# Hybrid decoder layer on one core: other start addresses in SBUF for matmul operands, no work on the empty state, and a square root in the last rows

## The chip, the cores and the metric

The kernel runs on one core of a Trainium2 chip. The metric is device time in microseconds. TensorE (PE) multiplies, with its weight loads shown apart as PEld; VectorE (DVE), ScalarE (ACT) and GpSimd (POOL) do the elementwise work; SyncE (SP) issues DMAs. SBUF is the memory on the chip that all of them read, PSUM the one that TensorE writes.

## The reference

A layer for 2048 tokens of width 1024, float32:

```
u    = rmsnorm(x) * w_mix
proj = u @ w_in
# 4 HGRN2 heads of 128: a gated linear recurrence, computed in chunks
S_t  = diag(f_t) S_{t-1} + k_t v_t^T ;  o_t = S_t^T q_t ;  S_0 = 0
# 8 attention heads of 64, 2 key/value heads, window 128, a sink logit per head
h    = x + concat(rmsnorm(o_hg) * silu(g), o_att) @ w_out
v    = rmsnorm(h) * w_ffn
gate = causal_conv3(v @ w_gate) + conv_b          # 2816 channels
h    = h + (silu(gate) * (v @ w_up)) @ w_down
out  = rmsnorm(h) * w_final
```

The state S starts empty, so the first chunk has no product with it, and the state after the last chunk is not needed.

## The kernel before

**Precision.** Large products are computed from a high and a low part of each operand (both of type float32r, `split_into`: a cast on ScalarE, a subtraction on VectorE). A product is thus a triple of matmuls: high weight by high input, high weight by low input, low weight by high input (lines 734 to 736 in gate and up, 921 to 923 in down, 202 in the projections). Each loads a weight block of 128 columns and streams 512 columns.

**Stages.** The tokens are taken in two halves of 1024 (`hf`). Each half goes through the heads and attention (`hgrn`, `attend`; their stages are woven together by the list `ORDER`), the output projection (`out_proj`), gate and up (`gate_up`: 11 pairs of feature tiles, each with one gate unit and one up unit) and `down`.

**Gate, up and down by Strassen's scheme.** A unit of two feature tiles and two halves of tokens is made of seven products instead of eight (`pair_unit`). Their weights are the blocks A11, A12, A22, the difference S3, and the combinations S1, S2 and S4, which `prep_pair` makes on VectorE. A11, A12, S3 and A22 lie in ring buffers `whi` and `wlo`. The combinations are allotted by the helper `m` from the slots of tag `m`, eight of 1024 floats, which other tiles (`x`, the heads' q, the residual `h`, `y`, one weight pair of the output projection) also use: `S` holds the sums, `Sh` and `Sl` the high and low parts of S1 and S2, `S4` both parts of S4. (The profile calls these `S`, `Sh`, `Sl` and, for `S4`, `S` again.) The first pair of each half uses other homes: the buffers `ga` for `Sh` and `Sl`, and `dd`. `down` uses the two `ga` buffers as a third home for weights, `gad`, high part in the first and low part in the second.

**Where a tile starts.** A pool lays its tiles one behind another in each partition, so a tile's start follows from the sizes of those before it, rounded up to 32 bytes. In the built program before, the tiles that 512-wide matmuls read start 64 bytes past a multiple of 128, except: the second `ga` buffer (96 past), `dd` (0 past). From `F64` in the heads' pool on, starts are 32 past, which holds for `v`, `SS`, `sc` and the scores' `qh` and `ql`.

**The state.** `hgrn` transposes K by chunks into `Kn` (`pkn`), multiplies by v (`pu`), and accumulates in `SS`; the output `po` of a chunk adds the product of Q with the state before it. Before, this is done for all eight chunks of both halves, with a zeroed `state` at first.

**The last rows.** `last_rows` makes the last products of the second half by rows of 128 tokens (`tb` 0 to 3): ScalarE squares and sums a row block, VectorE forms the inverse root by an integer estimate and three Newton steps on 128x1 tiles, and scales the rows on their way out.

Within this, the scheduler of the language's tile layer sets each engine's final order from data dependences and its own timing model.

Of the kernel before, what the change touches and what calls it, by code (L numbers as in the profile page):

```python
# [17 lines left out]
P = 128  # L18
D = 1024
KT = D // P  # L20
S = 2048
HALF = 1024
NH = S // HALF
TT = HALF // P
# [5 lines left out]
FT = FF // P  # L30
EPS = 1e-6
PIECES = [2, 2, 2, 2, 2, 1]
OPS = ["B11", "T1", "B21", "T2", "T3", "B22", "T4"]
QUADS = ["A11", "A12", "A21", "A22"]
PRODUCTS = [("P1", "A11", "B11"), ("P5", "S1", "T1"), ("P6", "S2", "T2"), ("P3", "S4", "B22"),
            ("P7", "S3", "T3"), ("P2", "A12", "B21"), ("P4", "A22", "T4")]
AFTER = {2: 'po'}
ORDER = ("f0 q0 l0 qa0 v0 s0 sc0 w0 pv0 p0 f1 q1 l1 g0 pw0 w1 qa1 g1 sc1 f2 s1 q2 p1 qa2 m0 pv1 pw1 l2 v1 "
         "s2 sc2 f3 m5 q3 g2 p2 pv2 pw2 qa3 m6 m1 sc3 l3 m4 m2 s3 g3 pv3 p3 pw3").split()
UP_AFTER = 'T2'  # L40
LEVELS = [1, 2, 4, 8, 16, 32, 64]
NEG = -1.0e30
UT = 7
# [5 lines left out]
def hymba_layer(ctx: ExitStack, tc: tile.TileContext, a: dict, out: bass.AP, rows_out: bass.AP):  # L49
    nc = tc.nc  # L50
# [6 lines left out]
    cp = pool("const")  # L57
    xp = pool("x")
    wp = pool("w")
    hp = pool("h")  # L60
# [13 lines left out]
        return [(b, slice(b * 512, (b + 1) * 512)) for b in range(NB)]  # L74


    nmw = cp.tile([P, KT], F32, name="nmw")
    nc.scalar.dma_start(nmw, a["norm_mix_w"])
    ones = cp.tile([P, P], F32, name="ones")
    nc.vector.memset(ones, 1.0)  # L80
    warm = cp.tile([P, 1], F32, name="warm")
    nc.scalar.activation(warm, ones[:, 0:1], AF.Sigmoid)
    ident = cp.tile([P, P], F32, name="ident")
    nc.gpsimd.memset(ident, 1.0)
    nc.gpsimd.affine_select(out=ident, in_=ident, compare_op=ALU.is_equal, fill=0.0,
                            base=0, pattern=[[-1, P]], channel_multiplier=1)
    state = cp.tile([P, HG, P], F32, name="state")
    nc.vector.memset(state, 0.0)
    halo = cp.tile([P, FT, 2], F32, name="halo")
    nc.vector.memset(halo, 0.0)  # L90
    kc = cp.tile([P, 2, P], F32R, name="kcarry")
# [5 lines left out]
    marks = {}  # L97
# [350 lines left out]
    def hgrn(hf, h, X, invb, vs, WG, gates, mix, p, fu=None):  # L448

        fu = fu or unit(a["w_f"][h], X, "f")  # L450
        f = p.tile([P, HALF], F32, tag="f", name="f", bufs=2)
# [12 lines left out]
        Q = p.tile([P, HALF], F32, tag="Q", name="Q", bufs=2)  # L464
# [27 lines left out]
        F = f  # L492
        for m in LEVELS:
            nb = HALF // (2 * m)
            pl = ps("hg", "plev")
            if m < 32:
                n, nu = 64 // m, TT // 2
                far, near = [[512 - m, 2], [P, nu], [2 * m, n], [1, m]], [[512 + m, 2], [P, nu], [2 * m, n], [1, m]]
                G = p.tile([P, 512], F32, tag="G", name="G", bufs=2)
                nc.scalar.copy(across(G, 0, [[m, 2], [P, nu], [2 * m, n], [1, m]]), across(K, 0, near))  # L500
                for u in range(nu):
                    marks[m] = nc.tensor.matmul(across(pl, u * 64, [[256, 2], [1, 64]]), G[:, u * P:(u + 1) * P],
                                                across(Q, u * P + m, [far[0]] + far[2:]), start=True, stop=True)
                nf = P // m
                Kv, Qv = across(K, 0, near), across(Q, m, far)
                Fk = across(F, 1, [[4 * nf - 1, 2], [nf, nu], [2, n], [0, m]])
                Fq = across(F, 0, [[4 * nf + 1, 2], [nf, nu], [2, n], [0, m]])
                nc.vector.tensor_tensor(Kv, Kv, Fk, op=ALU.mult)
                nc.vector.tensor_tensor(Qv, Qv, Fq, op=ALU.mult)
            else:  # L510
                Qv = Q.rearrange("p (b w m) -> p b w m", w=2, m=m)
                Kv = K.rearrange("p (b w m) -> p b w m", w=2, m=m)
                for c in range(TT):
                    for s0 in range(0, P, 2 * m):
                        nc.tensor.matmul(pl[s0:s0 + m, c * m:(c + 1) * m], K[:, c * P + s0:c * P + s0 + m],
                                         Q[:, c * P + s0 + m:c * P + s0 + 2 * m], start=True, stop=True)
                Fv = F.rearrange("p (b w) -> p b w", w=2)
                nc.vector.tensor_tensor(Qv[:, :, 1], Qv[:, :, 1], Fv[:, :, 0:1].to_broadcast([P, nb, m]), op=ALU.mult)
                nc.vector.tensor_tensor(Kv[:, :, 0], Kv[:, :, 0], Fv[:, :, 1:2].to_broadcast([P, nb, m]), op=ALU.mult)
            Fv = F.rearrange("p (b w) -> p b w", w=2)  # L520
            Fn = p.tile([P, nb], F32, tag=f"F{m}", name=f"F{m}", bufs=1)
            nc.vector.tensor_tensor(Fn, Fv[:, :, 0], Fv[:, :, 1], op=ALU.mult)
            F = Fn
            if m < 32:
                mk = C.lmask[m].bitcast(U32).rearrange("p s t -> p (s t)")
                nc.vector.copy_predicated(across(ST.rearrange("p c t -> p (c t)"), m, far),
                                          across(mk, 0, [[64, 2], [0, nu], [m, n], [1, m]]),
                                          pl.rearrange("p (s u b m) -> p s u b m", s=2, u=nu, m=m))
                continue
            for s0 in range(0, P, 2 * m):  # L530
                nc.scalar.copy(ST[s0:s0 + m, :, s0 + m:s0 + 2 * m],
                               pl[s0:s0 + m, 0:TT * m].rearrange("p (c m) -> p c m", c=TT))
        yield
        v = vs[h]

        Kn = p.tile([P, TT, P], F32, tag="t4", name="Kn", bufs=2)
        for b in range(NB):
            pk = ps("hg", "pkn")
            for i in range(4):
                c = slice((b * 4 + i) * P, (b * 4 + i + 1) * P)  # L540
                nc.tensor.transpose(pk[:, i * P:(i + 1) * P], K[:, c], ident)
            nc.scalar.copy(Kn[:, 4 * b:4 * b + 4].rearrange("p a b -> p (a b)"), pk)
        SS = p.tile([P, TT, P], F32, tag="SS", name="SS", bufs=1)
        for b in range(NB):
            pu = ps("hg", "pu")
            for i in range(4):
                c = 4 * b + i
                marks["pu"] = nc.tensor.matmul(pu[:, i * P:(i + 1) * P], Kn[:, c], v[:, c], start=True, stop=True)
            for i in range(4):
                c = 4 * b + i  # L550
                prev = state[:, h] if c == 0 else SS[:, c - 1]
                nc.vector.scalar_tensor_tensor(SS[:, c], prev, F[:, c:c + 1], pu[:, i * P:(i + 1) * P],
                                               op0=ALU.mult, op1=ALU.add)
# [4 lines left out]
        po = [ps("hg", "po") for _ in range(NB)]  # L558
        for c in range(TT):
            cs = slice(c * P, (c + 1) * P)  # L560
            prev = state[:, h] if c == 0 else SS[:, c - 1]
            o = po[c // 4][:, c % 4 * P:(c % 4 + 1) * P]
            nc.tensor.matmul(o, ST[:, c], v[:, c], start=True, stop=False)
            marks["po"] = nc.tensor.matmul(o, Q[:, cs], prev, start=False, stop=True)
            nc.scalar.activation(on[:, c], o, AF.Square, accum_out=ss[:, c:c + 1])
        rs = rsqrt(ss, TT, 1.0 / P)
        if h == HG - 1:
# [6 lines left out]
        for b, bs in halves():  # L574
# [5 lines left out]
            else:  # L580
                nc.vector.scalar_tensor_tensor(blocks(g[:, bs]), blocks(pt, b), C.hgw, blocks(g[:, bs]),
                                               op0=ALU.mult, op1=ALU.mult)
            if h == HG - 1:
                hi, lo = mix[h]
                nc.scalar.copy(hi[:, bs], g[:, bs])
                nc.vector.tensor_tensor(lo[:, bs], g[:, bs], hi[:, bs].bitcast(F32), op=ALU.subtract)
        nc.vector.tensor_copy(state[:, h], SS[:, TT - 1])
        yield

    def project_v(hf, pr, X, rs, p):  # L590
# [91 lines left out]
    def prep_pair(src1, src2, home=None, ut=None, raws=None):  # L682
# [6 lines left out]
                    wp.tile([P, D], F32R, tag="lo", name="wlo", bufs=2))  # L689

        def m(name, shape=[P, D], dt=F32R):
            return hp.tile(shape, dt, tag="m", name=name, bufs=KT)

        A = None if home else ring()
        if A:
# [2 lines left out]
        if home:  # L698
            S1, S2, S4 = [ut(n) for n in ("S1", "S2", "S4")]
        else:  # L700
            S = m("S", [P, D], F32)
            S1, S2, S4 = S[:, lo], S[:, hi], r1[:, hi]
# [62 lines left out]
    def gate_up(hf, ops, hs, nxt, p):  # L765
# [5 lines left out]
        for pr in range(FT // 2):  # L771
            f0 = 2 * pr
            W, nxt = nxt, None
            ga = [p.tile([P, 2 + HALF], F32, tag="ga", name="ga", bufs=2) for _ in range(2)]

            def gate(i, j, x, y):
                dst = ga[i][:, 2 + j * 512:2 + (j + 1) * 512]
# [20 lines left out]
            for i in range(2):  # L798
# [3 lines left out]
                y = slot("y")  # L802
# [191 lines left out]
    def last_rows(hf, hh, st, fw, ready, pieces, p, then):  # L994
# [6 lines left out]
        def small(name):  # L1001
            return sp.tile([P, 1], F32, tag=name, name=name)

        for tb in range(4):
            ts = slice(tb * P, (tb + 1) * P)
            o = ps("mm", "rows")
# [27 lines left out]
            nc.scalar.activation(sq, o, AF.Square, accum_out=ss)  # L1034
            ms, mh, y, t = small("msr"), small("mhr"), small("yr"), small("tr")
            nc.vector.tensor_scalar(ms, ss, 1.0 / D, base[:, tb:tb + 1], op0=ALU.mult, op1=ALU.add)
            yi = y.bitcast(I32)
            nc.vector.tensor_scalar(yi, ms.bitcast(I32), 1, None, op0=ALU.logical_shift_right)
            nc.vector.tensor_scalar(yi, yi, -1.0, float(0x5F3759DF), op0=ALU.mult, op1=ALU.add)
            nc.vector.tensor_scalar(mh, ss, -0.5 / D, half[:, tb:tb + 1], op0=ALU.mult, op1=ALU.add)  # L1040
            for _ in range(3):
                nc.vector.tensor_scalar(t, y, y, mh, op0=ALU.mult, op1=ALU.mult)
                nc.vector.tensor_scalar(y, t, 1.5, y, op0=ALU.add, op1=ALU.mult)
            r = sq
# [130 lines left out]
```

## Time and profile before

| | |
|---|---|
| median of 3 runs | 2183.36 us (2181.68 to 2183.84) |
| the profiled execution | 2181.92 us |
| its span | 2179.9 us |
| granted TensorE clock, mean | 0.999 |
| TensorE busy | 2162.5 us, 99% |
| VectorE busy | 1630.9 us, 75% |
| ScalarE busy | 1049.7 us, 48% |
| HBM read, written | 195.37 MB, 57.15 MB |

"Busy" counts the time in which at least one instruction of an engine is under way. A group's row in the profile ends in count, busy time, mean duration of one in ns, and idle time of the engine just before. In the timeline a row begins with its start and its duration in us. A matmul is shown from its start to its modelled end, and the next one starts before that end; the time that a matmul takes of TensorE is the distance from one start to the next.

### The profile page before, as it was taken

What the parts mean: (1) busy time and instruction counts of PE and PEld (TensorE: products, weight loads), DVE (VectorE), ACT (ScalarE), POOL (GpSimd) and SP (SyncE); (2) the same over time, 40 slices, a digit from 0 to 9 for tenths busy, and PEclk for the clock granted to TensorE, in tenths of its full rate; (3) what the DMA queues carried; (4) which work ended last, traced back from release to release, by engine and by line L of the source; (5) the groups of instructions that cost most, each with busy time, mean ns of one, the idle gap of its engine ahead of it and who ended that gap; (6) DMA issues with size and microseconds to landing.
All of it is one profiled execution on the core that took longest, in us unless ns stands there. A gap on an engine that the chain in (4) does not pass through costs nothing.

```text
span 2179.9 us, 29020 instructions
## 1 busy us (share of the span) xinstructions
PE 2162.5 (99%) x11211; PEld 1813.3 (83%) x11211; DVE 1630.9 (75%) x2458; ACT 1049.7 (48%) x1825; POOL 15.8 (1%) x37
## 2 busy tenths in 40 slices
PE   8999999999999999999999999999999999999998
PEld 7988988888888888888889889888888888888887
DVE  6566668689787878785865666677888888787865
ACT  6445456554444445335635365445644444443452
POOL 2000000000000000000000000000000000000000
PEclk9999999999999999999999999999999999999999
DMA  4111112413232334964641010114232323259743
GB/s 156 40 30 39 30 39 69 135 59 126 92 115 93 99 118 152 384 227 152 205 135 30 30 49 22 50 61 143 70 116 87 129 84 124 86 190 393 232 145 131
DMA packets 91146, 254.41 MB, mean 117 GB/s; under 512 B 11136, under 2 KB 13952, under 8 KB 91008
## 3 DMA queue, kind: packets, MB, share of 16 engines
q1 hardware_dynamic: 90576, 252.29, 34.6%
q8 instruction: 88, 1.44, 0.3%
q14 instruction: 50, 0.41, 0.1%
q10 hardware_dynamic: 432, 0.27, 0.0%
HBM read 195.37 MB, written 57.15 MB: 116 GB/s over the span
## 4 chain that ended last, share of the span: by engine, by line
PE 97%; DVE 1%; ACT 1%; DMA 1%; issue 0%; SPq 0%; DVEq 0%
PE pop L202 8%; PE X L734 7%; PE X L735 7%; PE X L736 7%; PE q L202 4%; PE g L202 4%; PE f L202 4%; PE hq L202 4%; PE Y L735 4%; PE Y L734 4%; PE Y L736 4%; PE pdx L922 3%; PE pdx L921 3%; PE pdx L923 3%; PE pdy L922 3%; PE pdy L921 3%
## 5 line engine op out<-in xcount | busy, mean ns | idle before, releaser
L609 ACT CAST whi<-raw 128x1024 fp32r<-128x1024 f32 x88 | 92.6, 1053 | 103.1 <-PE X L735 68.5
L805 DVE SCALAR_TENSOR_TENSOR y<-ga,cw,y 128x1024 f32<-128x1024 f32 x88 | 112.6, 1282 | 37.7 <-ACT y L803 37.7
L736 PE MATMUL X<-T,wlo 128*128 128x512 f32 x352 | 137.0, 389 | 0.0
L735 PE MATMUL X<-T,whi 128*128 128x512 f32 x352 | 136.9, 389 | 0.0
L734 PE MATMUL X<-T,whi 128*128 128x512 f32 x352 | 136.9, 389 | 0.0
L610 DVE TENSOR_TENSOR wlo<-raw,whi 128x1024 fp32r<-128x1024 f32 x88 | 107.5, 1221 | 5.7 <-ACT whi L609 5.7
L183 ACT CAST whi<-raw 128x1024 fp32r<-128x1024 f32 x58 | 60.6, 1050 | 102.6 <-PE g L202 22.4
L740 ACT COPY u<-X 128x512 f32<-128x512 f32 x88 | 51.8, 588 | 97.8 <-PE X L736 97.7
L610 DVE TENSOR_TENSOR xld<-raw,xhd 128x1024 fp32r<-128x1024 f32 x72 | 81.1, 1133 | 8.1 <-ACT xhd L609 7.9
L609 ACT CAST xhd<-raw 128x1024 fp32r<-128x1024 f32 x72 | 69.5, 979 | 32.5 <-DMA raw<-act1B 9.6
L202 PE MATMUL pop<-XH,wlo 128*128 128x512 f32 x256 | 83.7, 392 | 0.8 <-DVE wlo L184 0.8
L202 PE MATMUL pop<-XL,whi 128*128 128x512 f32 x256 | 83.8, 391 | 0.0
L202 PE MATMUL pop<-XH,whi 128*128 128x512 f32 x256 | 83.4, 396 | 0.2
L184 DVE TENSOR_TENSOR wlo<-raw,whi 128x1024 fp32r<-128x1024 f32 x58 | 70.4, 1218 | 12.3 <-ACT whi L183 12.3
L734 PEld LDWEIGHTS X<-T,whi 128*128 128x128 f32 x352 | 66.1, 188 | 13.8
L735 PEld LDWEIGHTS X<-T,whi 128*128 128x128 f32 x352 | 66.1, 188 | 13.7
L736 PEld LDWEIGHTS X<-T,wlo 128*128 128x128 f32 x352 | 66.1, 188 | 13.7
L740 ACT COPY s<-X 128x512 f32<-128x512 f32 x44 | 25.9, 590 | 106.3 <-PE X L736 106.3
L602 PE MATMUL pvv<-whi,XL 128*128 128x256 f32 x256 | 73.5, 289 | 0.0
L601 PE MATMUL pvv<-whi,XH 128*128 128x256 f32 x256 | 73.1, 287 | 0.0
L603 PE MATMUL pvv<-wlo,XH 128*128 128x256 f32 x256 | 72.1, 284 | 0.0
L734 PE MATMUL X<-T,Sh 128*128 128x512 f32 x176 | 68.7, 390 | 0.0
(389 smaller groups left out, 6555.6 us busy)
## 6 DMA issues: line engine op xcount, KB each, us to landing
wr<-in_w_down SPq DMA_DIRECT2D x90, 512.0 KB, 5.3
raw<-in_w_gate SPq DMA_DIRECT2D x44, 512.0 KB, 3.6
raw<-in_w_up SPq DMA_DIRECT2D x44, 512.0 KB, 3.6
raw<-act0T SPq DMA_DIRECT2D x20, 512.0 KB, 5.7
raw<-act1T SPq DMA_DIRECT2D x20, 512.0 KB, 5.0
act0B<-y SPq DMA_DIRECT2D x33, 256.0 KB, 2.3
act1B<-y SPq DMA_DIRECT2D x33, 256.0 KB, 2.2
raw<-in_w_out SPq DMA_DIRECT2D x16, 512.0 KB, 3.6
```

The source lines that it names most:

```text
L202: nc.tensor.matmul(o[b], w, x[:, bs], start=f, stop=l)
L601: nc.tensor.matmul(o[:, 0:256], xh[:, t], hi[:, c], start=kt == 0, stop=False)
L602: nc.tensor.matmul(o[:, 0:256], xl[:, t], hi[:, c], start=False, stop=False)
L609: nc.scalar.copy(h, src)
L610: return (eng or nc.vector).tensor_tensor(l, src, h.bitcast(F32), op=ALU.subtract)
L734: nc.tensor.matmul(o, wh[:, ws], xh, start=i == 0 and not more, stop=False, skip_group_check=more)
L735: nc.tensor.matmul(o, wh[:, ws], xl, start=False, stop=False, skip_group_check=more)
L736: nc.tensor.matmul(o, wl[:, ws], xh, start=False, stop=i == 3, skip_group_check=more)
L740: nc.scalar.copy(t, o)
L805: nc.vector.scalar_tensor_tensor(y, g[:, w:w + HALF], C.cw[:, ft, w:w + 1], y, op0=ALU.mult, op1=ALU.add)
L921: nc.tensor.matmul(o, wh[:, i, c], ah[:, i, cols], start=f, stop=False, skip_group_check=more)
L922: nc.tensor.matmul(o, wh[:, i, c], al[:, i, cols], start=False, stop=False, skip_group_check=more)
```

## The change

1. The small tiles `nmw` and `warm`, and the tiles `F64`, become larger, and `ga` buffers get 4224 bytes instead of 4104. In the built program the tiles that matmuls read in the heads, `ga`'s second buffer and `dd` now start 64 bytes past a multiple of 128.
2. The slots of tag `m` are 4128 bytes apart instead of 4096, and their eight starts are 64, 96, 0, 32, 64, 96, 0 and 32 past a multiple of 128. `Sl` and `S4` begin 16 bytes into theirs.
3. The first chunk of the first half makes no product with the state, and the last chunk of the second half makes no transpose, product, sum or copy of the state. The memset of `state` goes.
4. In the last rows, the integer estimate and two of three Newton steps give way to a square root on ScalarE and a reciprocal on VectorE, with a warm-up of the root at the start of `last_rows`.

```diff
+GA = 1056
-    nmw = cp.tile([P, KT], F32, name="nmw")
+    nmw = cp.tile([P, 16], F32, name="nmw")[:, 0:KT]
-    warm = cp.tile([P, 1], F32, name="warm")
+    warm = cp.tile([P, 32], F32, name="warm")[:, 0:1]
-    nc.vector.memset(state, 0.0)
...
-            Fn = p.tile([P, nb], F32, tag=f"F{m}", name=f"F{m}", bufs=1)
+            Fn = p.tile([P, max(nb, 16)], F32, tag=f"F{m}", name=f"F{m}", bufs=1)[:, 0:nb]
...
+        kept = TT if hf + 1 < NH else TT - 1
-            for i in range(4):
+            n = min(4, kept - 4 * b)
+            for i in range(n):
...
+                if hf == 0 and c == 0:
+                    nc.vector.tensor_copy(SS[:, 0], pu[:, 0:P])
+                    continue
...
-            nc.tensor.matmul(o, ST[:, c], v[:, c], start=True, stop=False)
-            marks["po"] = nc.tensor.matmul(o, Q[:, cs], prev, start=False, stop=True)
+            empty = hf == 0 and c == 0
+            marks["po"] = nc.tensor.matmul(o, ST[:, c], v[:, c], start=True, stop=empty)
+            if not empty:
+                marks["po"] = nc.tensor.matmul(o, Q[:, cs], prev, start=False, stop=True)
...
-        nc.vector.tensor_copy(state[:, h], SS[:, TT - 1])
+        if hf + 1 < NH:
+            nc.vector.tensor_copy(state[:, h], SS[:, TT - 1])
...
         def m(name, shape=[P, D], dt=F32R):
-            return hp.tile(shape, dt, tag="m", name=name, bufs=KT)
+            o = 4 if name in ("Sl", "S4") else 0
+            t = hp.tile([P, D + 8], dt, tag="m", name=name, bufs=KT)[:, o:o + D]
+            return t if len(shape) == 2 else t.rearrange("p (a b) -> p a b", a=2)
...
-            ga = [p.tile([P, 2 + HALF], F32, tag="ga", name="ga", bufs=2) for _ in range(2)]
+            ga = [p.tile([P, GA], F32, tag="ga", name="ga", bufs=2)[:, 0:2 + HALF] for _ in range(2)]
...
+        nc.scalar.activation(warm, ones[:, 0:1], AF.Sqrt)
         for tb in range(4):
...
-            yi = y.bitcast(I32)
-            nc.vector.tensor_scalar(yi, ms.bitcast(I32), 1, None, op0=ALU.logical_shift_right)
-            nc.vector.tensor_scalar(yi, yi, -1.0, float(0x5F3759DF), op0=ALU.mult, op1=ALU.add)
+            nc.scalar.activation(t, ms, AF.Sqrt)
+            nc.vector.reciprocal(y, t)
             nc.vector.tensor_scalar(mh, ss, -0.5 / D, half[:, tb:tb + 1], op0=ALU.mult, op1=ALU.add)
-            for _ in range(3):
+            for _ in range(1):
```

The order on three engines. ScalarE at the start, before:

```order
L78 DMA nmw<-in_norm_mix_w 128x8
L82 ACT_TABLE_LOAD
L82 ACTIVATE warm<-ones 128x1
L292 CAST whi<-raw 128x512
L216 ACTIVATE XH<-x,nmw 128x512 x2
```

and now:

```order
L79 DMA nmw<-in_norm_mix_w 128x8
L83 ACT_TABLE_LOAD
L83 ACTIVATE warm<-ones 128x1
L1014 ACT_TABLE_LOAD
L1014 ACTIVATE warm<-ones 128x1
L292 CAST whi<-raw 128x512
L216 ACTIVATE XH<-x,nmw 128x512 x2
```

Nothing in the program waits for the root's warm-up (line 1014), and the scheduler has moved it, with its table load, from the last rows to the front, ahead of the first cast of weights.

TensorE in the first half, at the first chunk of the first head's output, where `po` is the output, `ST` the scores within the chunk, and the matmuls of the next head's `f` lie between; before:

```order
L387 MATMUL psc<-KS,ql 128x256
L202 MATMUL f_1202<-XH,wlo 128x512
L563 MATMUL po<-v,ST 128x128
L564 MATMUL po<-state,Q 128x128
L202 MATMUL f_1203<-XH,wlo 128x512
```

and now:

```order
L387 MATMUL psc<-KS,ql 128x256
L202 MATMUL f_1200<-XH,wlo 128x512
L569 MATMUL po<-v,ST 128x128
L202 MATMUL f_1201<-XH,wlo 128x512
L202 MATMUL f_1200<-XH,whi 128x512
```

The product with the state is gone, and what stood around it has stayed in its place.

VectorE at the end, for the last row block, where `msr` is the mean square and `yr` the inverse root; before:

```order
L1036 TENSOR_SCALAR msr<-ssr,base 128x1
L1040 TENSOR_SCALAR mhr<-ssr,half 128x1
L1038 TENSOR_SCALAR yr<-msr 128x1
L1039 TENSOR_SCALAR yr<-yr 128x1
L1042 TENSOR_SCALAR tr<-yr,mhr 128x1
L1043 TENSOR_SCALAR yr<-tr,yr 128x1
L1042 TENSOR_SCALAR tr<-yr,mhr 128x1
L1043 TENSOR_SCALAR yr<-tr,yr 128x1
L1042 TENSOR_SCALAR tr<-yr,mhr 128x1
L1043 TENSOR_SCALAR yr<-tr,yr 128x1
L1046 SCALAR_TENSOR_TENSOR sqr<-rows,yr,fw 128x256 x2
```

and now, with the root (line 1048) on ScalarE between the second and the third row:

```order
L1047 TENSOR_SCALAR msr<-ssr,base 128x1
L1050 TENSOR_SCALAR mhr<-ssr,half 128x1
L1049 RECIPROCAL yr<-tr 128x1
L1052 TENSOR_SCALAR tr<-yr,mhr 128x1
L1053 TENSOR_SCALAR yr<-tr,yr 128x1
L1056 SCALAR_TENSOR_TENSOR sqr<-rows,yr,fw 128x256 x2
```

On ScalarE the root's table is loaded once more, behind the squares of the second row block, and not again after:

```order
L1048 ACT_TABLE_LOAD
L1048 ACTIVATE tr<-msr 128x1 x2
L1045 ACTIVATE sqr,ssr<-rows 128x512
L1048 ACTIVATE tr<-msr 128x1
L1045 ACTIVATE sqr,ssr<-rows 128x512
L1048 ACTIVATE tr<-msr 128x1
```

Ten instructions in a row have become five on VectorE, with one on ScalarE among them. The matmuls of gate and up stand in the same order as before; of their operands, only the addresses differ.

More of the change, by code (lines that the diff above doesn't have):

```diff
@@ L37 @@
 AFTER = {2: 'po'}
+UP_AFTER = 'T2'
 ORDER = ("f0 q0 l0 qa0 v0 s0 sc0 w0 pv0 p0 f1 q1 l1 g0 pw0 w1 qa1 g1 sc1 f2 s1 q2 p1 qa2 m0 pv1 pw1 l2 v1 "
          "s2 sc2 f3 m5 q3 g2 p2 pv2 pw2 qa3 m6 m1 sc3 l3 m4 m2 s3 g3 pv3 p3 pw3").split()
-UP_AFTER = 'T2'
 LEVELS = [1, 2, 4, 8, 16, 32, 64]
@@ L538, in hgrn @@
             pk = ps("hg", "pkn")
-            for i in range(4):
+            n = min(4, kept - 4 * b)
+            for i in range(n):
                 c = slice((b * 4 + i) * P, (b * 4 + i + 1) * P)
                 nc.tensor.transpose(pk[:, i * P:(i + 1) * P], K[:, c], ident)
-            nc.scalar.copy(Kn[:, 4 * b:4 * b + 4].rearrange("p a b -> p (a b)"), pk)
+            nc.scalar.copy(Kn[:, 4 * b:4 * b + n].rearrange("p a b -> p (a b)"), pk[:, 0:n * P])
         SS = p.tile([P, TT, P], F32, tag="SS", name="SS", bufs=1)
@@ L545, in hgrn @@
             pu = ps("hg", "pu")
-            for i in range(4):
-                c = 4 * b + i
+            for c in range(4 * b, min(4 * b + 4, kept)):
+                i = c % 4
                 marks["pu"] = nc.tensor.matmul(pu[:, i * P:(i + 1) * P], Kn[:, c], v[:, c], start=True, stop=True)
-            for i in range(4):
-                c = 4 * b + i
+            for c in range(4 * b, min(4 * b + 4, kept)):
+                i = c % 4
+                if hf == 0 and c == 0:
+                    nc.vector.tensor_copy(SS[:, 0], pu[:, 0:P])
+                    continue
                 prev = state[:, h] if c == 0 else SS[:, c - 1]
```

## The prediction

> **What bounds the kernel now.** I read the page's totals and chain first, then the waits of TensorE, then single matmuls in the timeline.
>
> ```profile
> span 2179.9 us, 29020 instructions
> PE 2162.5 (99%) x11211; PEld 1813.3 (83%) x11211; DVE 1630.9 (75%) x2458; ACT 1049.7 (48%) x1825; POOL 15.8 (1%) x37
> PEclk9999999999999999999999999999999999999999
> PE 97%; DVE 1%; ACT 1%; DMA 1%; issue 0%; SPq 0%; DVEq 0%
> ```
>
> The chain that ended last is TensorE for 97% of the span, and the granted clock (third line) stays at its top figure. What does TensorE wait for?
>
> ```profile
> PE kv L202 <- ACT XH L216: 5.7, 1, 5.7
> PE pu L548 <- ACT Kn L542: 1.1, 1, 1.1
> ```
>
> These are the two longest of seven kinds of wait, and all seven sum to 9.3 us, 5.7 of it at the very start. So the time of this kernel is the number of matmuls times the distance from one start to the next. VectorE, ScalarE and the queues have slack nearly everywhere; an edit there costs only at the start and after the last matmul. Everything therefore turns on that distance, and on whether the addresses change it.
>
> The busy time per matmul is no distance, since matmuls overlap, but it already tells groups of one shape apart:
>
> ```profile
> L735 PE MATMUL Y<-B,S 128*128 128x512 f32 x168 | 65.4, 389 | 0.0
> L736 PE MATMUL Y<-B,dd 128*128 128x512 f32 x8 | 3.2, 395 | 0.0
> L922 PE MATMUL pdx<-xld,hid 128*128 128x512 f32 x168 | 65.4, 389 | 0.0
> L922 PE MATMUL pdx<-xld,gad 128*128 128x512 f32 x96 | 38.3, 399 | 0.0
> ```
>
> A mean of 389 ns is the rule; `gad` and `dd` stand out with 399 and 395. In the built program nearly all operands of the 512-wide matmuls start 64 bytes past a multiple of 128. The exceptions are few: the low part of each `gad` weight (96 past, because its neighbour `ga` is 4104 bytes long), the `dd` of the first pair (0 past), and the low part `Sl` of the first pair (96 past). The slow groups and the odd addresses are the same tiles. Now the distances, in the last down-projection, 15 aligned matmuls and then 24 with `gad`:
>
> ```profile
> 2125.65 0.39 PE L921 MATMUL pdy<-xhd,hid 128*128 128x512 f32 x1
> ...
> 2129.05 0.39 PE L921 MATMUL pdy<-xhd,gad 128*128 128x512 f32 x1
> ...
> 2129.74 0.40 PE L921 MATMUL pdy<-xhd,gad 128*128 128x512 f32 x1
> 2129.97 0.40 PE L922 MATMUL pdy<-xld,gad 128*128 128x512 f32 x1
> 2130.21 0.39 PE L923 MATMUL pdy<-xhd,gad 128*128 128x512 f32 x1
> 2130.44 0.40 PE L921 MATMUL pdy<-xhd,gad 128*128 128x512 f32 x1
> ...
> 2134.64 0.40 PE L921 MATMUL pdy<-xhd,hid 128*128 128x512 f32 x1
> ...
> 2135.33 0.39 PE L921 MATMUL pdy<-xhd,hid 128*128 128x512 f32 x1
> ```
>
> Aligned: 3.40 us for 15, so 227 ns each and 680 a triple (high by high, high by low, low by high part). With `gad`, from 2129.74 to 2134.64: 4.90 us for 7 triples, 700 ns each. Only one weight load of the three is off, yet the triple loses 20 ns, and most of it on the matmul during which that load runs (2129.97 to 2130.21, 240 ns). After the last one the next aligned triple still takes 690 (2134.64 to 2135.33). Now `dd`, where all three loads of a triple are off, by 64:
>
> ```profile
> 470.28 0.40 PE L734 MATMUL Y<-B,dd 128*128 128x512 f32 x1
> ...
> 473.08 0.39 PE L734 MATMUL X<-T,whi 128*128 128x512 f32 x1
> ...
> 474.47 0.39 PE L734 MATMUL X<-T,whi 128*128 128x512 f32 x1
> ```
>
> Twelve matmuls in 2.80 us: 700 ns a triple again, and the six aligned ones behind them take 1.39 us, 30 ns over 6 x 227. Two different patterns of offset, one price: 20 ns a triple, and 10 to 30 ns more on the way back.
>
> **The change part by part.**
>
> *Aligned now.* `ga` slots of 4224 bytes put the low part of `gad` at 64 past: 208 triples x 20 ns = 4.2 us gained. `dd` and `Sl` of the first pairs: 8 and 16 triples x 20 ns = 0.5 us. All of it is TensorE time, so it counts in full.
>
> *Off now.* The slots of tag `m` are 4128 bytes apart, so their starts step through 64, 96, 0 and 32 past a multiple of 128, and `Sl` and `S4` lie 16 bytes further: 80, 112, 16 and 48. In the built program the products with `S1`, `S2` and `S4` of the 42 later gate and up units, 504 triples, now have at least one load that is off; in 432 all three are, in 72 the low part alone: 3 x 432 + 72 = 1368 loads. None of these mixtures is in the trace. Bounds: nothing, or even a gain, if an offset kept throughout a run is harmless. The nearest row for that is the attention scores, whose weights lie 32 past:
>
> ```profile
> L387 PE MATMUL psc<-KS,ql 128*128 128x256 f32 x120 | 30.3, 282 | 0.0
> L602 PE MATMUL pvv<-whi,XL 128*128 128x256 f32 x256 | 73.5, 289 | 0.0
> ```
>
> They are not slower than the aligned matmuls of the same width (282 against 289). At 7 ns a load the gain would be 1368 x 7 = 9.6 us. From above: if each load that is off cost by itself what the one in `gad` does, 1368 x 20 = 27.4 us. I take the price that both 512-wide patterns show, 20 ns a triple: 504 x 20 = 10.1 us, because width 512 with three matmuls a weight block is what these products are. To it come the ways back: in the built order some 90 stretches end in aligned matmuls, at 10 to 30 ns, so 0.9 to 2.7; I take 1.8. Together 11.9 us lost.
>
> *Other addresses.* One of the output projection's eight units has its weights in such slots, 16 triples: 0.3 lost. The 240 scores of width 256 move from 32 past to 64 past; by the rows above between 0 and 7 ns each, so 0 to 1.7: I take 0.5.
>
> *Left out on TensorE.* Four transposes (last chunk of the second half), the four state products that follow, and the four products with an empty state; each fp32 product is two passes. Distances from merged rows:
>
> ```profile
> 1360.73 0.93 PE L541 MATMUL pkn<-ident,K 128*128 128x128 f32 x7
> 1365.22 1.95 PE L548 MATMUL pu<-v,Kn 128*128 128x128 f32 x16
> ```
>
> (1.95 - 0.28) / 15 = 0.11 us a pass and as much a transpose: 4 x 0.11 + 16 x 0.11 = 2.2 us gained. (`v` in `pu` lies 32 past and `K` in `pkn` 64 past, at the same distance, so the small products that move from 32 to 64 past are costed at nothing.) The `SS` updates and state copies that go with them were on VectorE beside matmuls and gain nothing.
>
> *The start.* The root's warm-up was moved by the scheduler behind the first one, so a second table load stands ahead of the first cast:
>
> ```profile
> 1.24 1.28 ACT L82 ACT_TABLE_LOAD   x1 [1.24 <-PEq L1161]
> 3.75 0.62 ACT L292 CAST whi<-raw 128x512 fp32r<-128x512 f32 x1 [1.01 <-DMA raw<-in_w_att]
> 4.90 1.58 ACT L216 ACTIVATE XH<-x,nmw 128x512 fp32r<-128x512 f32 x2 [0.53 <-DMA x<-in_xP]
> ```
>
> The cast moves from 3.75 to some 4.25 us, ends at 4.87, and the next step waits until 4.90 for its DMA anyway: nothing, at most 0.5 if that DMA comes earlier. The memset of `state` goes from an idle VectorE: nothing.
>
> *The end.* After the last matmul the inverse root stands alone:
>
> ```profile
> 2172.50 0.60 ACT L1034 ACTIVATE sqr<-rows 128x512 f32<-128x512 f32 x1 [7.52 <-issue]
> 2173.61 0.15 DVE L1038 TENSOR_SCALAR yr<-msr 128x1 int32<-128x1 int32 x1
> 2173.99 0.27 DVE L1042 TENSOR_SCALAR tr<-yr,mhr 128x1 f32<-128x1 f32 x1
> 2174.54 0.27 DVE L1042 TENSOR_SCALAR tr<-yr,mhr 128x1 f32<-128x1 f32 x1
> 2175.10 0.27 DVE L1042 TENSOR_SCALAR tr<-yr,mhr 128x1 f32<-128x1 f32 x1
> 2175.66 0.91 ACT L1050 ACTIVATE y<-y,yr 128x256 f32<-128x256 f32 x2 [2.47 <-DVE yr L1043]
> L411 ACT ACTIVATE es<-es 128x8 f32<-128x8 f32 x16 | 3.4, 210 | 17.0 <-DVE es L404 16.9
> ```
>
> Two Newton steps less: 2 x 0.56 = 1.1 us. The two integer steps (2173.61 to 2173.99, 0.4) give way to a square root on ScalarE (0.21 by the last row), a hop back and a reciprocal of some 0.2: 0.6. Net 0.9 gained. The order shows the table for the root loaded in the first row block, while VectorE still works on other sums, so not in the end. A load there would cost 1.28 us.
>
> *Sum.* 11.9 + 0.3 + 0.5 - 4.2 - 0.5 - 2.2 - 0.9 = +4.9 us on the profiled execution's 2181.9 us (span 2179.9 and 2.0 around it). The median of the runs is 2183.4, 1.5 above; there the same step gives 2188.3.
>
> **The rivals.**
>
> *An offset kept through a run is harmless in gate and up (faster).* For it: the scores at 32 past. Against it: `dd`, twelve loads at one offset and slow to the last. Without the 11.9 the sum is -7.0: 2176.4. It decides below 7.0 us for the 504 triples, 14 ns each.
>
> *Only loads at multiples of 32 pay; those 16 further are free.* Then 264 triples with the high part at 0, 32 or 96 pay: 5.3 and some 0.9 for ways back, -0.8 in all: 2182.6. The trace has no load at 16 past to speak against it.
>
> *Each load that is off pays for itself.* By 2129.97 to 2130.21 that is 13 ns a load: 1368 x 13 = 17.8, net +10.8, 2194.2; with 20 ns it would be 2203.8. Against it: `dd`, 7 ns a load.
>
> *Addresses do nothing at all.* The Trainium skill's "TensorE: Matmul & The Clock Gate" (Part 2, step by step) says that TensorE has two independent read ports, so that loading the next weights takes no read bandwidth from the running matmul. As a mechanism of this kernel: neither the 4.7 gained nor the 12.7 lost exist, and only 2.2 + 0.9 remain, 2180.3. The `gad` rows stand against it: 20 ns go exactly where the odd load runs.
>
> **How the numbers follow.** Some 0.2% (4.4 us) is what a measurement of this kernel tells from no change. My forecast: 0.45; each load by itself: 0.15; harmless: 0.20; multiples of 32 alone: 0.15; nothing: 0.05. The forecast lies at that bound, so somewhat over half of it counts as slower. Slower: 0.27 + 0.15, with rounding 0.43. Faster: 0.18 of the harmless case and some of the next two, 0.22. The rest, 0.35, is no change. The range runs from the harmless case, 2176, to beyond the 13 ns case, 2199, and leaves out its 20 ns variant and a gain as large as that of the scores. The forecast's own range is 2185 to 2192, by the ways back and the scores.
>
> **What would show it.** Right: `gad` triples fall from 700 to 680 ns; triples with `S`, `Sh` and `Sl` rise from 680 to about 700, and A11, A12 and A22 products right behind them by 10 to 30 ns once; the end from the last matmul shortens by 0.9 us. Wrong: gate and up triples that stay at 680, or go beyond 710; a table load after the last matmul; a TensorE wait that the new order brings, since I costed the reordering at nothing on the strength of 9.3 us of waits in all.

## The result, and the profile after

The changed kernel takes 2186.35 us (median of 18 runs, 2185.70 to 2188.85), the kernel before 2182.52 us in the runs beside it (18 runs, 2181.68 to 2186.22). The ratio is 1.0018, with a 95% interval of 1.0011 to 1.0024: slower by 3.8 us, 2.4 to 5.2 by the interval. That is about what separates a change from none here. Behind it stand larger parts with opposite signs. The profiled execution took 2185.7 us, with a span of 2183.6.

The page's totals and the chain, of the changed kernel:

```profile
span 2183.6 us, 28950 instructions
PE 2168.3 (99%) x11191; PEld 1812.1 (83%) x11191; DVE 1625.9 (74%) x2429; ACT 1045.1 (48%) x1828; POOL 14.5 (1%) x37
PEclk9999999999999999999999999999999999999999
PE 98%; DVE 1%; DMA 0%; issue 0%; SPq 0%; ACT 0%; DVEq 0%; ACTq 0%
```

TensorE has 20 matmul instructions fewer than before and is busy 5.8 us longer, at the same granted clock (third line). It is still the chain. None of its waits has grown by more than 0.2 us, and one of 1.1 us is gone, so the distance between matmuls must have grown. The groups of TensorE by line, operation and tile (count, then busy time in us and mean ns of one) show where:

```profile
L745 PE MATMUL X<-T,whi 128*128 128x512 f32 x352 | 137.1, 389 | 0.0
L744 PE MATMUL X<-T,Sh 128*128 128x512 f32 x176 | 69.7, 396 | 0.0
L746 PE MATMUL X<-T,Sl 128*128 128x512 f32 x176 | 69.4, 394 | 0.0
L744 PE MATMUL Y<-B,S 128*128 128x512 f32 x168 | 66.0, 393 | 0.0
L932 PE MATMUL pdx<-xld,hid 128*128 128x512 f32 x168 | 65.4, 389 | 0.0
L931 PE MATMUL pdx<-xhd,gad 128*128 128x512 f32 x96 | 37.4, 389 | 0.0
L932 PE MATMUL pdx<-xld,gad 128*128 128x512 f32 x96 | 38.0, 395 | 0.0
L933 PE MATMUL pdx<-xhd,gad 128*128 128x512 f32 x96 | 37.2, 397 | 0.0
```

`whi` and `hid` stand at 389 as before. `Sh`, `Sl` and `S`, whose slots moved, have risen to 393 to 396. `gad` was to fall to 389 as well, and has not: high by low was 399 and is 395, and low by high, 390 in the same group before, is 397. The slow matmuls have moved within the triple, and few have gone.

The timeline of TensorE shows it in distances. Two stretches of the gate and up products, each four triples with `S` and then the next product:

```profile
586.05 0.39 PE L744 MATMUL Y<-B,S 128*128 128x512 f32 x1
...
588.85 0.40 PE L744 MATMUL X<-B,whi 128*128 128x512 f32 x1
...
644.03 0.39 PE L744 MATMUL Y<-B,S 128*128 128x512 f32 x1
...
646.75 0.39 PE L746 MATMUL X<-B,wlo 128*128 128x512 f32 x1
```

The first takes 2.80 us, 700 ns a triple. The second takes 2.72, 680 ns, as if nothing had moved. In the built program the weights of the first lie 112 bytes past their moving operand, counted modulo 256, those of the second 16. (This distance, the start of the weights less that of the moving operand, modulo 256, is called the offset from here on.) And seven triples with `gad`:

```profile
2134.58 0.39 PE L931 MATMUL pdy<-xhd,gad 128*128 128x512 f32 x1
...
2139.43 0.39 PE L931 MATMUL pdy<-xhd,hid 128*128 128x512 f32 x1
```

4.85 us, 693 ns each; it was 700 and was to be 680. Both parts of `gad` now lie 64 past a multiple of 128, but with slots of 4224 bytes (16.5 x 256) the low part is at offset 128.

The end after the last matmul and the start (start us, us, engine, line, operation):

```profile
2.75 1.28 ACT L1014 ACT_TABLE_LOAD   x1
4.16 0.60 ACT L292 CAST whi<-raw 128x512 fp32r<-128x512 f32 x1
5.05 1.34 ACT L216 ACTIVATE XH<-x,nmw 128x512 fp32r<-128x512 f32 x2 [0.29 <-DMA x<-in_xP]
...
2177.43 0.60 ACT L1045 ACTIVATE sqr<-rows 128x512 f32<-128x512 f32 x1 [6.47 <-PE rows L1043]
2178.40 0.20 ACT L1048 ACTIVATE tr<-msr 128x1 f32<-128x1 f32 x1 [0.28 <-DVE msr L1047]
2178.63 0.16 DVE L1049 RECIPROCAL yr<-tr 128x1 f32<-128x1 f32 x1
2178.83 0.27 DVE L1052 TENSOR_SCALAR tr<-yr,mhr 128x1 f32<-128x1 f32 x1
2179.39 0.91 ACT L1060 ACTIVATE y<-y,yr 128x256 f32<-128x256 f32 x2 [0.79 <-DVE yr L1053]
```

From the squares to the scaling the end takes 1.96 us (2177.43 to 2179.39), against 3.16 before (2172.50 to 2175.66). There is no table load in it. The cast starts at 4.16 and its successor still waits for a DMA.

Summed over the program, from the start of each matmul to the start of the next:

| matmuls | before, us | after, us | difference | forecast |
|---|---|---|---|---|
| gate and up, 3696 | 838.9 | 848.1 | +9.2 | +11.4 |
| down, 1716 | 393.4 | 391.9 | -1.5 | -4.2 |
| projections with the output's, 2496 | 587.3 | 587.5 | +0.2 | +0.3 |
| products of the last rows, 132 | 31.2 | 31.1 | -0.1 | 0 |
| small ones | 315.8 | 312.5 | -3.3 | -1.7 |
| from the last squares to the scaling | 3.16 | 1.96 | -1.2 | -0.9 |

(Forecast of the first row: 11.9 - 0.5; of the small ones: 0.5 - 2.2.)

### The profile page after: what moved, and what is told of

Its sections match the earlier page's. It is cut to its first block, busy times and chain, and to the rows that moved or that the text cites. A ratio compares the mean times of both kernels' runs of the same rounds, so it can differ in the third digit from the quotient of the medians.

```text
span 2183.6 us, 28950 instructions
## 1 busy us (share of the span) xinstructions
PE 2168.3 (99%) x11191; PEld 1812.1 (83%) x11191; DVE 1625.9 (74%) x2429; ACT 1045.1 (48%) x1828; POOL 14.5 (1%) x37
## 4 chain that ended last, share of the span: by engine, by line
PE 98%; DVE 1%; DMA 0%; issue 0%; SPq 0%; ACT 0%; DVEq 0%; ACTq 0%
PE pop L202 8%; PE X L744 7%; PE X L745 7%; PE X L746 7%; PE q L202 4%; PE g L202 4%; PE hq L202 4%; PE f L202 4%; PE Y L744 4%; PE Y L745 4%; PE Y L746 4%; PE pdx L933 3%; PE pdx L932 3%; PE pdx L931 3%; PE pdy L933 3%; PE pdy L932 3%
## 5 line engine op out<-in xcount | busy, mean ns | idle before, releaser
L183 ACT CAST whi<-raw 128x1024 fp32r<-128x1024 f32 x58 | 60.5, 1048 | 96.8 <-PE g L202 20.2
```

## Experiments

Three questions were open: which part of the change makes which difference, by what rule an address costs, and whether the parts add up. Each kernel was timed beside the kernel before, whose medians were 2182.14, 2182.08 and 2181.97 in the three sets.

**The slots of gate and up alone.** In the changed kernel, the slots of tag `m` go back to 4096 bytes:

```diff
-            o = 4 if name in ("Sl", "S4") else 0
-            t = hp.tile([P, D + 8], dt, tag="m", name=name, bufs=KT)[:, o:o + D]
-            return t if len(shape) == 2 else t.rearrange("p (a b) -> p a b", a=2)
+            return hp.tile(shape, dt, tag="m", name=name, bufs=KT)
```

> The changed kernel with the slots of tag m back at 4096 bytes and no 16 bytes ahead of Sl and S4; everything else as changed. The trace of the changed kernel has gate and up 9.2 us longer from start to start than before and the output projection 0.2 to 0.4. Theory (weights that lie off cost time where they are loaded): all of it comes back, so 9.5 us under the changed kernel, near 2177, and faster than before by some 5.5 us. Rival (the difference in gate and up has another cause, such as the new order or slower writes into the tiles): gate and up keep a good part of the 9.2 us and the kernel stays above 2180.

2176.51 us (2175.86 to 2177.96), ratio 0.9972 (0.9961 to 0.9983). So the slots cost 9.8 us in the changed kernel, and the rest of the change gains. `Sh` and `S` are back at 390 and 389 ns.

**`GA` at a multiple of 256 bytes.** Slots of 4352 bytes put the low part of `gad` at offset 0:

```diff
-GA = 1056
+GA = 1088
```

> The changed kernel with ga buffers of 4352 bytes instead of 4224, so that the low part of gad starts 4352 bytes (17 x 256) behind the high part instead of 4224 (16.5 x 256). Theory A (what counts is the distance of the loaded weights from the streamed operand modulo 256): the 208 gad triples fall from 693 to 680 ns, 2.7 us in all. Theory B, that of the prediction (modulo 128): nothing changes in down, and the time is that of the changed kernel.

2183.36 us (2182.96 to 2185.47), ratio 1.0005 (0.9996 to 1.0014): 3.0 less than the changed kernel. The groups of `gad` by line, of this run:

```profile
L932 PE MATMUL pdx<-xld,gad 128*128 128x512 f32 x96 | 37.3, 389 | 0.0
L933 PE MATMUL pdx<-xhd,gad 128*128 128x512 f32 x96 | 36.4, 389 | 0.0
```

395 and 397 have become 389. The period is not 128.

**Both.**

```diff
-GA = 1056
+GA = 1088
...
-            o = 4 if name in ("Sl", "S4") else 0
-            t = hp.tile([P, D + 8], dt, tag="m", name=name, bufs=KT)[:, o:o + D]
-            return t if len(shape) == 2 else t.rearrange("p (a b) -> p a b", a=2)
+            return hp.tile(shape, dt, tag="m", name=name, bufs=KT)
```

> Slots of 4096 bytes and ga buffers of 4352: every 512-wide matmul has its weights at a multiple of 256 bytes from what it streams. Theory A: 9.5 + 2.7 us under the changed kernel, near 2174, some 8 us faster than before. Theory B: no faster than with the slots put back alone, near 2177.

2174.11 us (2172.81 to 2174.88), ratio 0.9961 (0.9949 to 0.9974), 12.2 less than the changed kernel (9.8 + 3.0 for the two apart). Every 512-wide matmul is now at offset 0, and this kernel beats both others. The runs below start from it.

**Everything 64 bytes further.** The first tile of the first pool is twice as wide, so all operands move together:

```diff
-    nmw = cp.tile([P, 16], F32, name="nmw")[:, 0:KT]
+    nmw = cp.tile([P, 32], F32, name="nmw")[:, 0:KT]
```

> As e3_both, with one small tile at the front 64 bytes longer, so that all operands start 0 instead of 64 past a multiple of 128 and the distances between them stay. Theory A (distances alone count): the time of e3_both within 1 us. Rival C (the place itself counts, 64 past a multiple of 128 being the good one): the 2680 triples of width 512 each lose 20 ns as dd did, 50 us more.

2173.49 us (2172.68 to 2175.18), ratio 0.9960 (0.9946 to 0.9973). The 512-wide operands now start at multiples of 128, and nothing changes. "64 bytes past a multiple of 128" is no good place in itself; what counts, by this run, is places against each other.

**The weights of gate and up at 64 and at 128.** Two kernels put the pool that holds the slots of tag `m` 64 or 128 bytes further, with a second gap behind it, so that later pools stay where they were modulo 256:

```diff
+    gap = pool("gap")
+    gap.tile([P, 16], F32, name="gap")   # 32 for 128 bytes
     hp = pool("h")
+    gap2 = pool("gap2")
+    gap2.tile([P, 48], F32, name="gap2")   # 32 for 128 bytes
```

> As e3_both, but the pool that holds the slots of tag m begins 64 bytes later (and what follows is put back by another gap), so that the weights of S1, S2 and S4 lie 64 bytes off in all three loads: 504 triples in gate and up and 32 in the output projection. Theories A (modulo 256) and B (modulo 128) both: the 20 ns a triple of dd, 10.1 us, and 10 to 30 ns for each of some 90 ways back, so 11 to 13 us over e3_both. Rival (an offset kept through a run is harmless): nothing.

> As e5, with a gap of 128 bytes instead of 64. Theory A (modulo 256): a cost, estimated from the 13 ns a triple that gad shows in the changed kernel with its low part 128 off, at 504 x 13 = 6.6 us and up to 12. Theory B (modulo 128): the time of e3_both.

At 64: 2187.40 us (2185.85 to 2189.46), ratio 1.0020 (1.0010 to 1.0029), 13.3 over the kernel at offset 0. At 128: 2186.71 us (2185.77 to 2190.11), ratio 1.0021 (1.0012 to 1.0030), 12.6 over it. Both are a little above what was expected (11 to 13, and 6.6 to 12). By a period of 128 the second would have cost nothing. The groups of the run at 128:

```profile
L746 PE MATMUL X<-T,Sh 128*128 128x512 f32 x176 | 69.9, 397 | 0.0
L746 PE MATMUL Y<-B,S 128*128 128x512 f32 x168 | 66.5, 396 | 0.0
```

By distances, a triple with all three loads off took 700 ns on average at 64 and 698 at 128, where one at offset 0 takes 680. With the low part alone off by 128 (`gad` in the changed kernel) it took 693. The whole of gate and up grew by 12.2 and 12.3 us in the sums, from 838.6.

**All of them 16 bytes off, and 144.** The slots are 4352 bytes and the tiles lie 16 (or 144) bytes into each; to make room, a scratch area for DMA descriptors was halved:

```diff
-            return hp.tile(shape, dt, tag="m", name=name, bufs=KT)
+            t = hp.tile([P, D + 64], dt, tag="m", name=name, bufs=KT)[:, 4:4 + D]   # 36:36 + D for 144
+            return t if len(shape) == 2 else t.rearrange("p (a b) -> p a b", a=2)
```

> As e3_both, but the weights of S1, S2 and S4 start 16 bytes into slots of 4352 bytes, so that all three loads of the 504 triples lie 16 off; the scratch at the start of SBUF is 1024 bytes shorter to make room. The changed kernel's trace has three-load runs at 16, 144 and 240 off in which a triple takes 680 ns. Theory A with that row: nothing, the time of e3_both. Theory B as predicted (every load that is off costs): 10 to 12 us over e3_both.

> As the run with all sum slots 16 bytes in (slots of 4352 bytes), but 144 bytes in: S, Sh, Sl and S4 of the 42 later gate and up units lie 144 past the moving operand modulo 256, and nothing else moves. Theory A: the few triples of the changed kernel at 144 (680 ns) are the rule, and 144 is free as 16 is, though 128 costs 15 ns a triple: 2174, within 1 us. Theory B: only places near 0 modulo 256 are free and those triples were too few or stood in good company: 504 triples at 15 to 20 ns, 7.6 to 10.1 us more: 2182 to 2184.

At 16: 2174.26 us (2173.02 to 2175.10), ratio 0.9958 (0.9941 to 0.9975). At 144: 2173.82 us (2173.00 to 2174.95), ratio 0.9962 (0.9948 to 0.9976). Both are free. A steady triple takes 680 ns (median) in both, and the group of the run at 144 reads as at offset 0:

```profile
L743 PE MATMUL X<-T,Sh 128*128 128x512 f32 x176 | 68.7, 390 | 0.0
```

So an offset costs or not by its value: 128 costs 18 ns a triple on average, 144 nothing.

**The moving operand instead of the weights.** A gap of 128 bytes between the rings of the high and the low activations. The weights of the projections, of gate and up and of down stay in place modulo 256:

```diff
+    gaps = []
     def new_x():
-        return (xp.tile([P, HALF], F32R, tag="xh", name="XH", bufs=KT),
-                xp.tile([P, HALF], F32R, tag="xl", name="XL", bufs=KT))
+        hi = xp.tile([P, HALF], F32R, tag="xh", name="XH", bufs=KT)
+        if not gaps:
+            gaps.append(xp.tile([P, 32], F32, tag="g1", name="g1", bufs=1))
+        lo = xp.tile([P, HALF], F32R, tag="xl", name="XL", bufs=KT)
+        if len(gaps) < 2:
+            gaps.append(xp.tile([P, 32], F32, tag="g2", name="g2", bufs=1))
+        return hi, lo
```

> The kernel with 4096-byte slots and GA of 1088, with a gap of 128 bytes between the rings of the high and the low parts of the activations, and one behind them. Every weight keeps its address modulo 256; only the streamed low parts move by 128. Of each triple one load then runs beside a stream at 128: in 2020 triples (832 pairs of L202's projections, 704 of gate and up, 484 of down). Theory A: what counts is the distance between the weights that are loaded and the operand that streams meanwhile: 14 ns a triple, as where only the low weight was 128 off (694 instead of 680), up to 20: 28 to 40 us more, 2202 to 2214. Theory B: what counts is where the weights lie, among themselves or against a fixed line: no change, 2174.

2188.60 us (2187.23 to 2189.71), ratio 1.0028 (1.0017 to 1.0038): 14.5 over the kernel at offset 0. That is far from no change, so the weights' own addresses don't decide; and it is half of what theory A expected, or less. The groups say why:

```profile
L749 PE MATMUL X<-T,whi 128*128 128x512 f32 x352 | 136.9, 389 | 0.0
L750 PE MATMUL X<-T,whi 128*128 128x512 f32 x352 | 139.0, 395 | 0.0
L751 PE MATMUL X<-T,wlo 128*128 128x512 f32 x352 | 136.6, 388 | 0.0
L937 PE MATMUL pdx<-xld,gad 128*128 128x512 f32 x96 | 37.9, 395 | 0.0
```

Of each triple only the middle matmul is slow, the one through which the moved operand streams, and single triples in the timeline put it at 234 ns against 227:

```profile
649.89 0.39 PE L749 MATMUL X<-T,whi 128*128 128x512 f32 x1
650.11 0.40 PE L750 MATMUL X<-T,whi 128*128 128x512 f32 x1
650.35 0.39 PE L751 MATMUL X<-T,wlo 128*128 128x512 f32 x1
650.57 0.39 PE L749 MATMUL X<-T,whi 128*128 128x512 f32 x1
```

Such triples take 687. With (704 + 484) x 7 ns = 8.3 us in gate, up and down, and 7.5 in the projections (588.3 to 595.8 in the sums), the parts come to 15.8; the two profiled executions are 15.5 apart.

The low activations are also weights in two places, so the expectation's "every weight keeps its address" does not hold there. In the last rows these are 44 loads (their products took 31.4 us instead of 31.1). In the products `pvv`, whose width is 256, they are the weights of 256 matmuls, which now lie at offset 128:

```profile
L617 PE MATMUL pvv<-whi,XL 128*128 128x256 f32 x256 | 72.8, 286 | 0.0
```

The mean was 289 before, at offset 0, and the distance to the next start is 118 ns here and 120 in the kernel at offset 0. At this width an offset of 128 cost nothing.

**The work on the empty state put back.**

```diff
+    nc.vector.memset(state, 0.0)
...
-        kept = TT if hf + 1 < NH else TT - 1
+        kept = TT
...
-                if hf == 0 and c == 0:
-                    nc.vector.tensor_copy(SS[:, 0], pu[:, 0:P])
-                    continue
...
-            empty = hf == 0 and c == 0
+            empty = False
```

(The copy of the last state stands outside its condition again, too.)

> The kernel with 4096-byte slots and GA of 1088 (2174.1 us), with the work on the empty state and on the unused last chunk put back: four transposes, eight fp32 state products, the copies and the memset. Theory A: TensorE is the whole path, so it costs the 20 passes of 0.11 to 0.14 us: 2.2 to 2.7, 2176.3 to 2176.8. Theory B: these products fell into waits for other engines and cost nothing: 2174.1. Theory C: the VectorE and ScalarE work that comes back with them delays TensorE as well: above 2178.

2176.54 us (2176.15 to 2178.32), ratio 0.9975 (0.9965 to 0.9985): 2.4 us over the kernel without that work. In its waits of TensorE stands a row that the kernel before has too and the changed one has not:

```profile
PE pu L551 <- ACT Kn L545: 1.1, 1, 1.1
```

It belongs to the second head of the second half. In the kernel before, the copies of `Kn` that its products `pu` need stood on ScalarE behind a table load (from 1282.14 us) and a step of `f`, and TensorE waited for them after four scores:

```profile
1283.97 1.06 ACT L542 COPY Kn<-pkn 128x512 f32<-128x512 f32 x2
1284.59 2.05 PE L548 MATMUL pu<-v,Kn 128*128 128x128 f32 x16 [1.05 <-ACT Kn L542]
```

In the changed kernel the scheduler has put them ahead, and the products start without a wait, in three parts with scores between them:

```profile
1278.29 0.59 ACT L544 COPY Kn<-pkn 128x512 f32<-128x512 f32 x1 [0.17 <-PE pkn L543]
1283.26 0.38 PE L550 MATMUL pu<-v,Kn 128*128 128x128 f32 x2
```

So the edit took away passes and, through the order on ScalarE, a wait that theory A did not have. In the sums of the two traces the small matmuls take 316.3 us with the work and 312.5 without: 2.8 of it in the transposes and the products with `Kn` and with the state, 1.1 in this wait. That is more than the 2.4 between the medians. The profiled execution with the work was the slowest of its nine, so 2.4 is the price that the medians show, and how it divides between passes and wait is read from the traces alone.

**The old inverse root put back.**

```diff
-        nc.scalar.activation(warm, ones[:, 0:1], AF.Sqrt)
...
-            nc.scalar.activation(t, ms, AF.Sqrt)
-            nc.vector.reciprocal(y, t)
+            yi = y.bitcast(I32)
+            nc.vector.tensor_scalar(yi, ms.bitcast(I32), 1, None, op0=ALU.logical_shift_right)
+            nc.vector.tensor_scalar(yi, yi, -1.0, float(0x5F3759DF), op0=ALU.mult, op1=ALU.add)
...
-            for _ in range(1):
+            for _ in range(3):
```

> The kernel with 4096-byte slots and GA of 1088 (2174.1 us), with the old inverse root of the last rows: shift, multiply-add and three Newton steps on VectorE, no square root and no warm-up for it. Theory A: the parts of the end and of the start are what the traces show, 1.2 us lost after the last matmul, 0.2 gained ahead of the first: 2175.1. Theory B: the end is set by the last transfer, whatever the root takes: no change, 2174.1. Theory C: the table load that the warm-up put ahead of the first cast cost more than the 0.2 shown, and the old root is no slower: below 2174.

2174.47 us (2174.28 to 2177.61), ratio 0.9968 (0.9955 to 0.9980), 0.4 over the kernel with the new root. The five runs scatter by more than the 1.0 to be told, so the medians do not decide between A and B. In the trace the end is what it was before:

```profile
2168.51 0.60 ACT L1042 ACTIVATE sqr<-rows 128x512 f32<-128x512 f32 x1 [7.52 <-issue]
2171.66 0.91 ACT L1058 ACTIVATE y<-y,yr 128x256 f32<-128x256 f32 x2 [2.47 <-DVE yr L1051]
```

3.15 us, 1.2 more than with the new root. Of the start: the first matmul began at 5.75 us here and at 5.67 in the kernel before, both without the second table load, and between 5.43 and 6.17 in the eleven traces with it. So the start has no price that these traces can tell.

## Why the prediction was right, step by step, and where not

The sum was +4.9 us, and the runs give +3.8, of the forecast's sign; 2186.35 us lies inside the forecast's own range of 2185 to 2192. That the sum is nearer than its terms is luck: the loss in gate and up was 2.2 us smaller than forecast and the small matmuls gained 1.6 more, while `gad` gained 2.7 less.

*TensorE's spacing is the time.* Right. The differences in the table add up to +3.3, the first matmul starts 0.15 later, and from the start of the last matmul to the squares it is 0.25 more, since the last one is now a 512-wide product and was a short transpose. That is the 3.7 by which the span grew.

*Off now, +11.9.* The mechanism and the sign are right, and so is the price of 20 ns where an offset costs in all of a triple: in the run at 64 it took 700 instead of 680. The term was too large: with the 0.3 of the output unit it was 12.2, and the run that undoes the slots alone gives 9.8. "At least one load that is off" was counted modulo 128 and by any value, yet some 55 of the 504 triples have offsets of 0, 16, 144 and 240 alone, and take 680. Most others take 687 to 703, two mixtures 706 and 707 (medians of each mixture). The ways back were at the low end of their 10 to 30 ns or under it: the first aligned triple behind products with one offset in all three loads lost 0 to 15 ns in the changed kernel, and 17 in the run at 64. The rival by which only multiples of 32 pay had seen the first half: 16 past is free. But 48, 80, 112, 176 and 208 cost 10 to 19 a triple, so a rule of 32 does not hold either.

*Other addresses, +0.3.* The output unit lies in such slots in both halves of the tokens, so it has 32 triples, not 16. The projections' +0.2 is too small to be told: their sum scatters from 587.2 to 590.6 us among traces with all of their weights at offset 0.

*Aligned now, -4.2 for `gad`.* This is the step that failed. `ga` slots of 4224 bytes "put the low part at 64 past" a multiple of 128, and the step took that for aligned. The period is 256: 64 and 192 past are 128 apart, and that costs 13 ns a triple. It gained 1.5 us, and the run with slots of 4352 bytes fetched 3.0 more. The trace of before could not tell 128 from 256, since no 512-wide operand there lay at an offset of 128; a bound for that should have been in the sum. The `dd` of the first pairs came to offset 0 and from 396 ns to 389, as forecast.

*The scores, +0.5.* The sums show those of width 256 shorter by 0.8, which is not the price of the address. With the empty state's work put back and the addresses of the changed kernel, they took 32.6 us, before 32.3. So the address costs some 0.3. The rest is the wait for `Kn`: it follows a score, so the distance from that score to the next start is 1.33 us in the kernel before, and 0.12 in the changed one.

*Left out on TensorE, -2.2.* Measured by the run that puts it back: 2.4. By the traces the distances from these transposes and products shrank by 2.8, and the wait of 1.1 us, which the prediction quoted as its second longest and left where it was, went too. That the new order was costed at nothing was the miss: it brought no wait, it took one away.

*The end, -0.9.* It was -1.2. The two Newton steps gave the 1.1. The root, the reciprocal and the two moves between the engines cost 0.05 more than the integer steps, where I allowed 0.2. And 0.14 came from the mean square, which starts 0.72 us after the squares instead of 0.86, since VectorE is free earlier. No table load fell there. *The start, 0:* right within what the traces tell.

*The rivals.* "Harmless" holds for a constant offset of 16 or 144, and fell with the run at 64, 13.3 us. "Each load pays for itself" fell with the triples: all three loads off cost 20 at 64 and 18 at 128, and the low one alone 13 at 128, no third of that. "Addresses do nothing" fell with every run that moved one operand against the other by 64 or 128. The Trainium skill's "TensorE: Matmul & The Clock Gate" (Part 2, step by step) says that the next weights load through a read port of their own and take no bandwidth from the running matmul. The 14.5 us of the run that moved nothing but the streamed operand, by 128 bytes, stand against that for these 512-wide matmuls of fp32r type. They show that the load and the running matmul affect each other's time; that it is read bandwidth that they share, they do not show.

What stays open is the mechanism. The rows at 128 fit an account by which a load at a costly offset slows two matmuls, the one beside which it runs and the one that uses it, by 5 to 7 ns each, and two such causes on one matmul do not add. In the run at 128 a matmul with its own weights at offset 0 and the next ones off took 232 ns, one with its own off and the next at 0 took 234, and one with both off 232 (medians). Other offsets do not fit it. In the kernel before, the low part of `gad` lay at offset 32, and the three matmuls of its triple took 233, 238 and 228 ns: the first, with no load off beside it, was slow, and the one that used the odd weights hardly so. In the run at 64 a matmul with its own weights at 0 and the next ones off took 226, no more than an aligned one. Why 16, 144 and 240 are free, and 128 is not, no run here explains, and no run was made with the weights at 32, 96, 160, 192 or 224 throughout.

## What to carry to other kernels

Where TensorE is the whole chain, compare groups of matmuls of one shape by mean time: a few that stand out by 5 to 10 ns can be a matter of addresses, and the built program tells which. Give weights and moving operands the same start modulo 256 (their distance counts; moving all of them by 64 changed nothing), and make every slot in a ring a multiple of 256 bytes. Before relying on a period that a trace suggests, ask which of its multiples the trace has really shown.

## What the runs showed of the hardware

- A 512-wide fp32r matmul follows the one before after 227 ns where the weights' start equals the moving operand's modulo 256, or lies 16, 144 or 240 past it; with all three loads of a triple 48, 64, 80, 112, 128, 176 or 208 past it takes 230 to 233 ns on average. (16, 64, 128 and 144 were run on 504 triples each; the others are the changed kernel's, 16 to 32 triples each.) With the low part alone 32 past, in the kernel before, a triple took 700 ns instead of 680.
- Moving every operand by 64 bytes together changes nothing (2173.49 against 2174.11 us); moving only the streamed low parts by 128 costs 14.5 us.
- At a width of 256, weights 128 past the moving operand cost nothing: 118 ns to the next start, against 120 at offset 0 (256 matmuls).
